# Expert passes in another order, weights in the mixers' scratch, and a ranking by small matmuls, in a two-block transformer kernel

## The chip, the core and the metric

The kernel runs on one core of a Trainium2 chip. A core has TensorE (PE, matmuls), VectorE (DVE), ScalarE (ACT), GpSimd (POOL) and SyncE (SP, which here issues nearly all transfers), an on-chip memory of 128 partitions (SBUF) and accumulation banks for matmuls (PSUM). Weights lie in the device's memory and are brought in by 16 DMA engines. The metric is the device time of one execution, in microseconds.

## What is computed

256 tokens of width 1024, in f32, go through two blocks. The first (attention or pooling, and a dense feed-forward) is not touched. The second has three token mixers with an output projection, then a mixture of 32 experts, then a gate with token inputs p:

```python
h = h + jnp.concatenate([ya, yb, yc], axis=-1) @ w_out[i]
h = h + hierarchical_moe(rms_norm_2(h, norm2_g[i]), router_gw[i], ...)
gate = jax.nn.sigmoid(rms_norm_2(h, ple_norm_g[i]) @ ple_gate_w[i])
h = h + gate * (p[i] @ ple_proj_w[i]).astype(F32)
return rms_norm_2(h, final_g)
```

The router takes the best of 4 groups for a token and in it the 2 best of 8 experts. Each expert has w_gate and w_up (1024 x 256) and w_down (256 x 1024), 1 MB each:

```python
g_top = jnp.argmax(g_logits, axis=-1)
e_val, e_loc = lax.top_k(e_in, TOP_K)
e_w = jax.nn.softmax(e_val, axis=-1) * g_w[:, None]
hb = jax.nn.silu(xb @ w_gate[e]) * (xb @ w_up[e])
yb = (hb @ w_down[e]) * wt[:, None]     # summed over a token's two experts
```

## The kernel before

The program runs `first_block`, then `second_mixers`, then `moe`. Engines run side by side, each in its own fixed order; semaphores hold an instruction until what it reads is there and what it overwrites has been read. A tile of a pool with the same name reuses the same buffer, so a load waits until the last reader of the former tile is done.

**Mixers.** `second_mixers` projects the tokens, runs the three mixers (scratch tiles kas, qa, sbt, uu, va and others) and multiplies with w_out (L1255). In its last stretch the rows are turned (L1282, L1324), and the router's logits are accumulated (L1283, L1325). `y_out` splits y into a high part (ACT, L1297) and a low part y - high (POOL, L1300), in two halves of 512 columns. Sixteen matmuls (L1344) multiply the token inputs p with ple_proj_w; their weights are loaded by L1267.

**Experts.** `moe` finds for each expert its tokens (one_hot, L1462, from the ranks rk), gathers their columns by matmuls with the one-hot matrix (`gather`, L1478, into xg, one gather for two passes) and works in passes (counted from 0) of 128 slots: the first matmuls of a pass (`hidden`, gate and up, L1588), the product with silu (L1594, ft), the turn of the hidden rows (L1616, into fh), the down projection (`down`, L1633), and the return to the tokens (`combine`, L1645, L1648). A pair holds two experts with 64 slots each, a quad four with 32 each. The first six experts (S) go by their number. The other 26 are ranked by their number of tokens: the six with most tokens (H) form pairs, the other 20 quads (Q). The order is SSSHHHQQQQQ: six pairs, five quads, eleven passes. Whatever does not fit in the slots is handled by an `If` after pass 7 (L1786), which reads a count nmi (L1748).

The ranking compares each of 26 counts with each (L1535 to L1545, 26 x 26 = 676 elements per partition on all 128 partitions), and puts ranks and weights of tokens in the new order (L1551, L1552). Its result `place` is read into a register of SP (L1406) for each load of a ranked expert.

**Loads.** `ExpertLoads.plan` lists 48 loads of 2 MB: (gate x, up x), (gate y, up y), (down x, down y) for a pair, six loads in the order gate, up, down for a quad. A load needs a place of 2 MB: three in the pool raw, three of whi and wlo, and at the start two of wx0 to wx3. `upto_pass(p, more)` issues loads up to so many beyond the end of pass p. All are issued by SP in program order (L1416), so a load that waits holds those behind it.

After the last pass a gate projection, sigmoid, the token inputs and a last norm end the kernel.

Of the kernel before, what the change touches and what calls it, by code (L numbers as in the profile page):

```python
# [19 lines left out]
P = 128  # L20
# [809 lines left out]
def w_consts(e, tp):  # L830
# [46 lines left out]
    def route():  # L877
# [6 lines left out]
        nc.gpsimd.memset(e.onb, 1.0)  # L884

# [32 lines left out]
def second_mixers(e, sp, ma, hx, xhi, xlo, racc):  # L918
# [3 lines left out]
    with tc.tile_pool(name="m2", bufs=1, reuse_waits="tile") as m2, banks(e, "psw", ps=3, z=3, py=1, px=1):  # L922
# [3 lines left out]
        kas = [m2.tile([P, 2, S], F32, name="ka%d" % j) for j in range(2)]  # L926
# [92 lines left out]
        def sgu_b():  # L1019
            vv = st["v"]  # L1020
            sq = m2.tile([P, 8, 64], F32, name="wd3")
# [39 lines left out]
        def sb1(i, s):  # L1061
# [5 lines left out]
            t = m2.tile([P, S + P], F32, name="sbt", bufs=3)  # L1067
# [13 lines left out]
        def sb3(i, s):  # L1081
# [8 lines left out]
            if s == 1:  # L1090
                if i == 0:
                    st["ya", 0] = m2.tile([P, S], F32, name="ya")
                elif i == 1:
                    t = m2.tile([P, 2, S], F32, name="vv")
                    st["ya", 1], st["ya", 2] = t[:, 0], t[:, 1]
# [61 lines left out]
        def ml3(h0, h1):  # L1157
            if h0 == 0:
                st["yb"] = m2.tile([P, 2, 384], F32, name="va")
# [11 lines left out]

        def p_load():
            st["p"] = [m2.tile([P, S], F32, name="qa", bufs=2) for _ in range(2)]
            for b in range(2):
                nc.gpsimd.dma_start(st["p"][b], a["p_2"][0, 0, b * P:(b + 1) * P])

        def p_turn():
            ps = bank(e, "z", [P, 2, S])
            for k in range(2):
                for b in range(2):  # L1180
                    nc.tensor.transpose(ps[:, k, b * P:(b + 1) * P], st["p"][b][:, k * P:(k + 1) * P], e.ident)
            e.pT = [e.tmp.tile([P, L], F32, name="acc2", bufs=2) for _ in range(2)]
            for k in range(2):
                nc.scalar.activation(e.pT[k][:, :S], ps[:, k], AF.Copy)
# [13 lines left out]
        u = st["u"] = m2.tile([P, 2, 256], F32, name="uu")  # L1198
# [7 lines left out]
        va = st["va"] = m2.tile([P, 2, 384], F32, name="va")  # L1206
# [9 lines left out]
        for i in range(3):  # L1216
            ps = col(("qa", i))
            qa = st["qa", i] = m2.tile([P, S], F32, name="qa", bufs=2)
# [13 lines left out]
        for f in (L_(sb1, 2, 1), L_(sb2, 2, 0), L_(sb3, 1, 1)):  # L1232
            f()
        plan_ = {
            (0, 0): [L_(decay, 3), L_(sb2, 2, 1), L_(sb3, 2, 0)], (0, 1): [L_(sb3, 2, 1), p_load],
            (1, 0): [ya_norm], (1, 1): [L_(conv_act, 0), L_(conv_act, 1)],
            (2, 0): [L_(ml1, 0), L_(ml1, 1), ya_out], (2, 1): [L_(conv_act, 2), L_(ml2, 0), L_(ml2, 1)],
            (3, 0): [L_(ml1, 2), p_turn], (3, 1): [L_(ml2, 2), L_(conv_act, 3)],
# [21 lines left out]
        for n in range(7):  # L1260
# [24 lines left out]
        def squares(ps, i0, i1, n):  # L1285

            for b in range(2):
                jk = m2.tile([P, 512], F32, name="wd3")
                nc.scalar.activation(jk[:, :(i1 - i0) * P], ps[b], AF.Square, accum_out=ssy[:, b, n:n + 1])

        def y_out(c, late=None):

            q = slice(c.start // KT, c.stop // KT)
            turned = lambda t, b: t[:, b].rearrange("p (k q) -> p k q", k=KT)[:, :, q]
            for b in range(2):
                src = y[:, b, c].rearrange("p (q k) -> p k q", k=KT)
                i = nc.scalar.activation(turned(yh, b), src, AF.Copy)  # L1297
                if late:
                    queue(e, i, late)
                nc.gpsimd.tensor_sub(turned(yl, b), src, fr(turned(yh, b)))  # L1300

        for i in range(KT + 2):
# [9 lines left out]
            if i == 6:  # L1312
# [3 lines left out]
                y_out(slice(0, 512))  # L1316
# [20 lines left out]

        e.pp = e.xs.tile([P, 2, D], F32, name="hs")
        for b in range(2):
            for hf in range(2):  # L1340
                c = slice(hf * 512, hf * 512 + 512)
                ps = bank(e, "z")
                for k in range(2):
                    nc.tensor.matmul(ps, e.pT[k][:, b * P:(b + 1) * P], e.proj[:, k, c], start=(k == 0), stop=(k == 1))  # L1344
# [564 lines left out]
```

## Time and profile before

| | us |
|---|---|
| median of 3 runs | 971.07 (969.52 to 971.22) |
| the profiled execution, device time | 970.93 |
| its span, first to last instruction | 969.1 |
| PE busy | 893.7 (92%) |
| DVE busy | 546.1 (56%) |
| ACT busy | 433.9 (45%) |
| POOL busy | 107.7 (11%) |

The device time is 1.83 us longer than the span, which covers only instructions. A busy share over the whole span mixes stages with different limits: 206.94 MB are read, 216 GB/s as a mean, but the rate changes from stage to stage, and so does what an engine waits for. Times below are counted from the start of the span. The first block ends near 530, the mixers near 677, the experts near 930.

### The profile page before, as it was taken

The page shows a single profiled execution, that of the slowest core. Times are in us where ns is not written, and L with a number is a line of the kernel's source. Part 1 is how long each engine was busy: PE and PEld are TensorE (multiplying, and loading weights), DVE is VectorE, ACT ScalarE, POOL GpSimd, SP SyncE. Part 2 cuts the span into 40 slices and gives each one's busy share as a digit, 9 for nine tenths or more (in the row PEclk, how much of TensorE's full clock was granted, in tenths as well). Part 3 has the DMA queues.
Part 4 walks back from the last instruction along what each step waited for, and adds up shares of the span by engine and source line. Part 5 has one row for each costly group of instructions (what it writes and reads, how often), then busy time and mean ns, then how long its engine had stood idle before and what let it go on. Part 6 is the DMA issues. An engine that isn't in the chain of part 4 may idle for free. (4 is left out here: it accounts for less than half of the span.)

```text
span 969.1 us, 16636 instructions
## 1 busy us (share of the span) xinstructions
PE 893.7 (92%) x6709; PEld 762.4 (79%) x6709; DVE 546.1 (56%) x1041; ACT 433.9 (45%) x800; POOL 107.7 (11%) x154
## 2 busy tenths in 40 slices
PE   7899999999999899999998899999799997778795
PEld 5799999998886899999998798899556563334355
DVE  7985555445998786655445755694933322221255
ACT  5564443435774574444433656564321220201155
POOL 3400000021400360000021310001100000000001
PEclk9899999999999999999999999999999997978898
DMA  7659543466332557553476135078795899999951
GB/s 233 208 174 217 175 147 120 127 216 248 121 111 88 174 124 226 179 171 120 130 234 220 65 118 182 7 260 303 295 385 228 357 414 417 419 415 415 412 180 44
DMA packets 110324, 210.24 MB, mean 217 GB/s; under 512 B 3660, under 2 KB 85776, under 8 KB 102048
## 3 DMA queue, kind: packets, MB, share of 16 engines
q1 hardware_dynamic: 108464, 204.91, 58.8%
q0 software_dynamic: 1488, 3.68, 2.1%
q8 instruction: 54, 0.88, 0.4%
q10 hardware_dynamic: 288, 0.52, 0.1%
q14 instruction: 30, 0.25, 0.1%
HBM read 206.94 MB, written 2.16 MB: 216 GB/s over the span
## 5 line engine op out<-in xcount | busy, mean ns | idle before, releaser
L315 DVE TENSOR_TENSOR wlo<-raw,whi 128x1024 fp32r<-128x1024 f32 (+4 forms) x151 | 213.9, 1420 | 119.8 <-ACT whi L315 119.4
L328 PE MATMUL ps<-xhi,whi 128*128 128x256 f32 (+1 forms) x912 | 261.6, 289 | 8.1 <-ACT xhi L319 5.3
L315 ACT ACTIVATE whi<-raw 128x1024 fp32r<-128x1024 f32 (+4 forms) x151 | 181.4, 1202 | 193.1 <-PE ps L328 188.8
L328 PE MATMUL ps<-xlo,whi 128*128 128x256 f32 (+1 forms) x912 | 261.7, 287 | 2.4 <-DVE xlo L320 1.9
L328 PE MATMUL ps<-xhi,wlo 128*128 128x256 f32 (+1 forms) x912 | 260.1, 285 | 0.0
L328 PEld LDWEIGHTS ps<-xhi,whi 128*128 128x128 f32 x912 | 173.4, 191 | 11.0 <-ACT xhi L319 6.1
L328 PEld LDWEIGHTS ps<-xlo,whi 128*128 128x128 f32 x912 | 173.9, 191 | 3.6 <-DVE xlo L320 2.6
L328 PEld LDWEIGHTS ps<-xhi,wlo 128*128 128x128 f32 x912 | 174.0, 191 | 0.0
L328 PE MATMUL ps<-hhi,whi 128*128 128x272 f32 (+1 forms) x352 | 100.9, 287 | 0.0
L328 PE MATMUL ps<-hhi,wlo 128*128 128x272 f32 (+1 forms) x352 | 100.4, 285 | 0.0
L328 PE MATMUL ps<-hlo,whi 128*128 128x272 f32 (+1 forms) x352 | 100.4, 285 | 0.0
L400 POOL TENSOR_TENSOR acc<-acc,sq 128x272 f32<-128x272 f32 (+1 forms) x24 | 34.6, 1442 | 373.0 <-ACT sq L394 372.6
L1594 DVE SCALAR_TENSOR_TENSOR ft<-ps,ws,ft 128x256 f32<-128x256 f32 x11 | 5.3, 483 | 114.8 <-PE ps L1588 79.8
L328 PEld LDWEIGHTS ps<-hhi,whi 128*128 128x128 f32 x352 | 66.9, 190 | 0.1
L328 PEld LDWEIGHTS ps<-hlo,whi 128*128 128x128 f32 x352 | 66.9, 190 | 0.1
L328 PEld LDWEIGHTS ps<-hhi,wlo 128*128 128x128 f32 x352 | 66.9, 190 | 0.0
L1588 PE MATMUL ps<-raw,xg 128*32 128x256 f32 (+1 forms) x512 | 51.5, 440 | 11.3 <-DMA raw<-in_w_up_dram 11.3
L1588 PEld LDWEIGHTS ps<-raw,xg 128*32 128x32 f32 (+1 forms) x512 | 30.4, 136 | 30.8 <-DMA raw<-in_w_up_dram 15.4
L1588 PE MATMUL ps<-whi,xg 128*32 128x256 f32 (+1 forms) x224 | 41.0, 456 | 9.6 <-ACTq L1786 5.8
L320 DVE SCALAR_TENSOR_TENSOR yl<-ps,ws,yh 128x512 fp32r<-128x512 f32 x22 | 16.5, 751 | 55.9 <-ACT yh L319 55.9
L423 DVE TENSOR_TENSOR ft<-ps,rpre 128x272 f32<-128x272 f32 (+1 forms) x44 | 18.8, 431 | 51.1 <-PE ps L328 51.0
L1588 PE MATMUL ps<-wlo,xg 128*32 128x256 f32 (+1 forms) x224 | 39.2, 453 | 5.1 <-DMA wlo<-in_w_gate_dram 5.1
(548 smaller groups left out, 1597.3 us busy)
## 6 DMA issues: line engine op xcount, KB each, us to landing
raw<-in_w_gate_up_dram SPq DMA_DIRECT2D x44, 1024.0 KB
raw<-in_w_up_dram SPq DMA_DIRECT2D x26, 1024.0 KB
raw<-in_w_down_dram SPq DMA_DIRECT2D x16, 1408.0 KB
raw<-in_w_down_dram SPq DMA_DIRECT2D x16, 1024.0 KB
whi<-in_w_gate_dram SPq DMA_DIRECT2D x14, 1024.0 KB
wlo<-in_w_gate_dram SPq DMA_DIRECT2D x10, 1024.0 KB
wlo<-in_w_down_dram SPq DMA_DIRECT2D x8, 1024.0 KB
whi<-in_w_down_dram SPq DMA_DIRECT2D x8, 1024.0 KB
```

What stands on the lines that cost most here:

```text
L315: return e.nc.scalar.activation(hi, src, AF.Copy), e.nc.vector.tensor_sub(lo, src, fr(hi))
L320: e.nc.vector.scalar_tensor_tensor(lo, src, g, fr(hi), op0=ALU.mult, op1=ALU.subtract))
L328: e.nc.tensor.matmul(ps, w(k), x(k), start=(first and n == 1), stop=(last and n == 3 * nk))
L400: nc.gpsimd.tensor_add(st["acc"][:, :n], st["acc"][:, :n], sq[:, :n])
L423: nc.vector.tensor_mul(t[:, :n], pss[0][:, :n], r[:, :n])
L1588: s.last = nc.tensor.matmul(pg[j][s.c * x:s.c * x + s.c], s.xg[:, k, s.s0 + x * s.c:s.s0 + (x + 1) * s.c], ws[x, j][:, k], start=(k == 0), ...
L1594: s.gated = nc.vector.scalar_tensor_tensor(t, pg[1], sc, t, op0=ALU.mult, op1=ALU.mult)
```

## The change

In words, in the order of the program:

- Some scratch of the mixers (kas, qa, sbt, u, va and one square) moves into two tiles wx0 and wx1 of the pool ma. Load 0 of the experts goes into these, and is issued by the mixers' plan behind the last use of sbt and va. With four tiles wx2 to wx5 of the pool mo for two more loads there are nine places for loads 0 to 17, seven for 18 to 31 and six from 32 on (`place_of`).
- `upto_pass` issues a load when the load before it in its place belongs to a pass that is over.
- The order of the passes is SSSQHQHQHQQ. Passes of one gather may now be a pair and a quad (`one_hot` with runs).
- The load of ple_proj_w and of p moves from the mixers behind pass 7, their matmuls from the mixers behind pass 8 (`token_inputs`, before pass 9).
- The low part of the second half of y moves from POOL to DVE, behind the one-hot of the first gather. That gather takes all high parts first and then the low parts.
- The ranking works on 26 partitions, with counts turned by a matmul against ones. Ranks and weights are turned (`by_expert`) and put in order by a matmul with the permutation (`in_place`). What only later passes need (`others`: weights in order, the count nmi) goes behind the first pass's turn. The small tiles of the router lie in one tile.
- ft and fh have one buffer instead of two; xg lies in two tiles of different pools.

```diff
+        w0, w1 = [ma.tile([P, 2048], F32, name="wx%d" % j) for j in range(2)]
+        kas = [w0[:, 512 * j:512 * j + 512].rearrange("p (s c) -> p s c", s=2) for j in range(2)]
...
-            (0, 0): [L_(decay, 3), L_(sb2, 2, 1), L_(sb3, 2, 0)], (0, 1): [L_(sb3, 2, 1), p_load],
+            (0, 0): [L_(decay, 3), L_(sb2, 2, 1), L_(sb3, 2, 0)], (0, 1): [L_(sb3, 2, 1), e.ml.load],
...
             if n == 3:
-                e.proj, _ = [sp.tile([P, 2, D], F32, name=t) for t in ("whi", "wlo")]
-                nc.sync.dma_start(e.proj, a["ple_proj_w_2"][0].rearrange("(k p) f -> p k f", p=P))
+                e.ml.load()
...
-                nc.gpsimd.tensor_sub(turned(yl, b), src, fr(turned(yh, b)))
...
-        y_out(slice(512, D), r)
-        e.ml.load()
+        e.y_low = y_out(slice(512, D), r)
...
+ORDER = "SSSQHQHQHQQ"
+NPASS = len(ORDER)
...
+    def halves(self, i):
+        if 1 <= i < 4:
+            t = self.e.raw.tile([P, 2, 2048], F32, name="raw")
+            return [t[:, 0], t[:, 1]]
+        if 4 <= i < 7:
             return [self.sp.tile([P, 2048], F32, name=n) for n in ("whi", "wlo")]
+        pool, i = (self.e.ma, 0) if i == 0 else (self.e.mo, 2 * i - 12)
+        return [pool.tile([P, 2048], F32, name="wx%d" % (i + j)) for j in range(2)]
+    def place_of(self, j):
+        return j % 9 if j < 18 else (j - 18) % 7 if j < 32 else (j - 32) % 6 + 1
...
-    def upto_pass(self, p, more=0):
-        while self.n < min(len(self.plan), self.upto[p] + more):
+    def upto_pass(self, p, short=0):
+        while self.n < len(self.plan) - short and self.prior(self.n) < self.upto[p]:
             self.load()
...
+            first = q == 0
+            if first:
+                pss = [bank(e, "ps", [P, 2, 256]) for _ in part]
+                for h in (hnh, hnl):
...
+        chosen = e.found
+        with tc.issue_after(chosen.ins):
+            e.y_low(nc.vector)
...
-            t = scratch()
-            nc.vector.tensor_tensor(t, over(key), down_(key), op=ALU.is_gt)
-            nc.vector.tensor_reduce(rank, t, axis=AX.X, op=ALU.add)
-            nc.vector.scalar_tensor_tensor(sorted_, over(rank), 1.0, down_(io[:, :ND]), op0=ALU.add, op1=ALU.is_equal)
...
+            nc.vector.scalar_tensor_tensor(key, key, keyc, e.ones[:ND, :ND], op0=ALU.is_gt, op1=ALU.mult,
+                                           accum_out=rankc)
+            nc.vector.tensor_scalar(perm, io[:ND, :ND], rankc, 1.0, op0=ALU.subtract, op1=ALU.is_equal)
+            ps = bank(e, "ps", [P, ND])
+            nc.tensor.matmul(ps[:1], e.ioc[:ND, 1:2], perm, start=True, stop=True)
...
+        def by_expert(src, n):
+            ps = bank(e, "ps", [P, 2, P])
             for b in range(2):
-                t = scratch(b)
-                nc.vector.tensor_mul(t, sorted_, over(src[:, b, NS:]))
-                nc.vector.tensor_reduce(to[:, b, NS:], t, axis=AX.X, op=ALU.add)
+                nc.tensor.transpose(ps[:ND, b], src[:, b, NS:], e.ident)
+            nc.scalar.activation(byx[:, n], ps[:ND].rearrange("p b t -> p (b t)"), AF.Copy)
+        def in_place(to, n):
+            ps = bank(e, "ps", [P, 2, ND])
+            for b in range(2):
+                nc.tensor.matmul(ps[:, b], byx[:, n, b * P:(b + 1) * P], perm, start=True, stop=True)
+            nc.vector.tensor_copy(to[:, :, NS:], ps)
...
+        def token_inputs():
+            pT = mo.tile([P, 2, S], F32, name="wx4")
+            pp = e.pp = mo.tile([P, 2, D], F32, name="wx5")
...
+        MID, LATE = 7, 8
...
-        in_place(rkq, rk)
-        in_place(wtq, wt)
+        for _ in range(2):
+            e.ml.load()
+        def others():
+            in_place(wtq, 1)
...
             if p == 0:
-                for n in range(2):
-                    e.ml.load([mo.tile([P, 2048], F32, name="wx%d" % (2 * n + j)) for j in range(2)])
...
             if p < last:
-                e.ml.upto_pass(p, 8 if p < 2 else 6)
+                e.ml.upto_pass(p)
...
+            if p == LATE:
+                token_inputs()
             if p == MID:
...
+                proj = mo.tile([P, 2, D], F32, name="wx2")
+                nc.sync.dma_start(proj, a["ple_proj_w_2"][0].rearrange("(k p) f -> p k f", p=P))
+                pin = mo.tile([P, 2, S], F32, name="wx3")
+                nc.gpsimd.dma_start(pin, a["p_2"][0, 0].rearrange("(b p) f -> p b f", p=P))
```

On SP, before, where the loads pass from static to ranked experts (wx2, wx3: load 7; raw_7688: load 8; raw_7691: load 9; nmi and place are reads into registers):

```order
L1416 DMA wx2_7684<-in_w_gate_2_dram 128x2048
L1416 DMA wx3_7685<-in_w_up_2_dram 128x2048
L1416 DMA raw_7688<-in_w_down_2_dram 128x2x1024 x2
L1748 TENSOR_LOAD nmi_7585
L1748 ISA x2
L1406 TENSOR_LOAD place_7530
L1406 ISA x2
L1416 ISA
L1416 DMA raw_7691<-in_w_gate_2_dram 128x2048
```

On SP now at the same place (wx4, wx5: load 8; wx0_7640, wx1_7641: load 9):

```order
L1424 DMA wx4_7494<-in_w_down_2_dram 128x2x1024
L1424 DMA wx5_7495<-in_w_down_2_dram 128x2x1024
L1414 TENSOR_LOAD place_7453
L1414 ISA x2
L1424 ISA
L1424 DMA wx0_7640<-in_w_gate_2_dram 128x2048
L1414 TENSOR_LOAD place_7453
L1414 ISA x2
L1424 ISA
L1424 DMA wx1_7641<-in_w_gate_2_dram 128x2048
L1826 TENSOR_LOAD nmi_7586
L1826 ISA x2
```

The read of nmi moved from ahead of load 9 to behind it, and the loads are one further: load 8 is the one in the last new place.

On SP, before, near the end of the mixers (raw_6467 and raw_6531: w_out; raw_6854: load 0; raw_6964: load 1):

```order
L148 DMA raw_6467<-in_w_out_2_dram 128x2x1024 x2
L148 DMA raw_6531<-in_w_out_2_dram 128x2x1024 x2
L1416 DMA raw_6854<-in_w_gate_2_dram 128x2048
L1416 DMA raw_6854<-in_w_up_2_dram 128x2048
L1416 DMA raw_6964<-in_w_gate_2_dram 128x2048
L1416 DMA raw_6964<-in_w_up_2_dram 128x2048
```

On SP now (raw_6461 and raw_6524: w_out; wx0_6701 and wx1_6702: load 0; raw_6844: load 1):

```order
L148 DMA raw_6461<-in_w_out_2_dram 128x2x1024 x2
L1424 DMA wx0_6701<-in_w_gate_2_dram 128x2048
L1424 DMA wx1_6702<-in_w_up_2_dram 128x2048
L148 DMA raw_6524<-in_w_out_2_dram 128x2x1024 x2
L1424 DMA raw_6844<-in_w_gate_2_dram 128x2048
L1424 DMA raw_6844<-in_w_up_2_dram 128x2048
```

Load 0 moved ahead of the second load of w_out.

On DVE, before, the ranking (key: counts; yh and so: 26 x 26 comparisons; gt, wp and ws belong to pass 0):

```order
L1535 SCALAR_TENSOR_TENSOR key<-ps,io 128x26
L1514 CAST wsp<-wt 128x3x2 x2
L1537 TENSOR_TENSOR yh<-key 128x676
L1515 TENSOR_TENSOR wsp<-wt,wsp 128x3x2 x2
L1538 TENSOR_REDUCE rank<-yh 128x26
L1601 CAST gt<-ps 128x256
L1539 SCALAR_TENSOR_TENSOR so<-rank,io 128x676
L1607 COPY wp<-ps 128x6
L1541 TENSOR_TENSOR yh<-so,io 128x676
L1609 TENSOR_TENSOR ws<-wp 128x3
L1551 TENSOR_TENSOR yl<-so,rk 128x676
```

On DVE now, from the selection slb on (tri_le: the ranks; qb: the low part of y; yl: small tiles; rankc and perm: ranks and permutation):

```order
L1462 TENSOR_TENSOR slb<-slb,yl 128x64
L1470 SCALAR_TENSOR_TENSOR tri_le<-ps,slb 128x64
L1491 TENSOR_TENSOR G<-io,tri_le 128x256 x2
L1291 TENSOR_TENSOR qb<-xlo,xhi 128x8x64 x2
L1581 SCALAR_TENSOR_TENSOR yl<-ps,io 26x26
L1583 SCALAR_TENSOR_TENSOR yl<-ps,ioc 26x1
L1544 TENSOR_TENSOR yl<-lgg,yl 128x8
L1547 TENSOR_TENSOR yl<-yl 128x8
L1585 SCALAR_TENSOR_TENSOR yl,rankc<-yl,ones 26x26
L1569 CAST wsp<-ss_7329 128x3 x2
L1587 TENSOR_SCALAR perm<-io,rankc 26x26
```

The operations of 676 elements are gone; the low part of y stands behind the one-hot G, and the ranking is done before the weights of the tokens.

## Rows read from the trace of the kernel before

**Rows 1.** The chain of waits: start, us, engine, line, tile

```profile
913.01 14.00 DMA wlo<-in_w_down_dram
...
927.05 3.62 PE ps L1633 x20
```

**Rows 2.** Stages: width, then PE, PEld, DVE, ACT, POOL busy, PEclk, DMA share, GB/s

```profile
767.00:927.00 160.00, 131.53 (x1066) 66.46 (x1065) 37.23 (x85) 26.04 (x53) 0.00 (x0) 0.88 1.02 412
...
699.00:767.00 68.00, 65.07 (x435) 41.11 (x434) 22.68 (x68) 16.94 (x33) 0.55 (x1) 0.97 0.79 310
...
636.00:699.00 63.00, 58.97 (x444) 52.17 (x442) 45.90 (x131) 30.45 (x69) 7.37 (x15) 0.97 0.77 292
...
600.00:630.00 30.00, 30.00 (x199) 26.41 (x198) 16.95 (x31) 16.28 (x27) 0.84 (x4) 1.00 0.02 5
```

**Rows 3.** Slices of 10 us, same columns

```profile
730.00:740.00 10.00, 10.00 (x70) 5.84 (x67) 4.56 (x13) 1.54 (x3) 0.00 (x0) 1.00 0.30 125
...
740.00:750.00 10.00, 10.00 (x83) 7.80 (x79) 3.06 (x6) 1.55 (x3) 0.00 (x0) 1.00 0.71 245
...
810.00:820.00 10.00, 7.00 (x64) 2.96 (x64) 0.00 (x0) 0.47 (x1) 0.00 (x0) 0.67 1.01 417
```

**Rows 4.** Waits of SP's queue: released by, us in total, times, longest

```profile
SPq L1416 <- PE ps L1588: 64.9, 12, 14.6
...
SPq L1416 <- PE ps L1633: 49.2, 12, 15.6
...
SPq L1748 <- DVE wp L1610: 4.3, 1, 4.3
```

**Rows 5.** SP's issues (loads 8 and 9): start, us

```profile
699.06 0.89 SPq L1416 DMA_DIRECT2D raw<-in_w_down_dram  x2
...
705.45 0.37 SPq L1416 DMA_DIRECT2D raw<-in_w_gate_dram  x1
```

**Rows 6.** Line L1089: duration ns, first and last start

```profile
L1089 PE MATMUL py<-sbt,va x12: 272/273/273, 590.6 to 620.2; 128*64 128x128 f32 x12
```

**Rows 7.** PE around the router and pass 0: start, us, [idle before]

```profile
676.34 5.40 PE L1344 MATMUL z<-whi,acc 128*128 128x512 f32 x12
...
684.78 0.19 PE L1445 MATMUL ps<-slb,ltb 128*128 128x32 bf16 x1 [3.05 <-DVE slb L1443]
...
691.91 7.18 PE L1588 MATMUL ps<-raw,xg 128*64 128x256 f32 x64
...
701.85 0.44 PE L1616 MATMUL ps<-ident,ft 128*128 128x128 f32 x2 [2.76 <-DVE ft L1594]
```

**Rows 8.** DVE around the router and in the ranking

```profile
679.07 0.16 DVE L1515 TENSOR_TENSOR wsp<-ss,wsp 128x3 fp32r<-128x3 f32 x1
...
679.62 1.48 DVE L1515 TENSOR_TENSOR wsp<-ss,wsp 128x3 fp32r<-128x3 f32 x1
...
681.16 1.47 DVE L1362 TENSOR_TENSOR ge<-ge,gi 128x8 f32<-128x8 f32 x1
...
693.39 0.86 DVE L1551 TENSOR_TENSOR yl<-so,rk 128x676 f32<-128x676 f32 x1
```

**Rows 9.** POOL around the router

```profile
679.56 3.04 POOL L1300 TENSOR_TENSOR qb<-xlo,xhi 128x512 fp32r<-128x512 f32 x2 [2.72 <-ACT xhi L1297]
```

**Rows 10.** Tile xlo on DVE: ns min, median, max

```profile
L1649 DVE TENSOR_TENSOR xlo<-xlo,ps x44: 674/679/689, 716.0 to 933.9; 128x512 f32<-128x512 f32 x44
```

**Rows 11.** PE, hidden matmuls of passes 3, 5, half of 6 (from 0)

```profile
740.41 7.13 PE L1588 MATMUL ps<-raw,xg 128*64 128x256 f32 x64
...
772.86 7.13 PE L1588 MATMUL ps<-raw,xg 128*64 128x256 f32 x64
...
795.42 3.83 PE L1588 MATMUL ps<-raw,xg 128*32 128x256 f32 x63
```

**Rows 12.** Lines L1344 and L1786

```profile
L1344 PE MATMUL z<-whi,acc x16: 592/592/676, 673.0 to 681.1; 128*128 128x512 f32 x16
...
L1786 PEldq COMPARE_BRANCH  x1: 6107/6107/6107, 839.6 to 839.6; - x1
```

More of the change, by code (lines that the diff above doesn't have):

```diff
@@ L1336, in second_mixers, with first_max @@
                                                op0=ALU.mult, op1=ALU.add)
[L1338 to L1344, printed above, removed]
[L1345 to L1350 removed]
+        e.y_low = y_out(slice(512, D), r)
+def first_max(e, small, src, n, iota):
     nc = e.nc
     m = src.shape[1]
[L1354 removed]
+    mx = small(m)
     nc.vector.tensor_reduce(mx, src, axis=AX.X, op=ALU.max)
[L1356 removed]
+    eq = small(m, n)
     nc.vector.tensor_tensor(eq, src, mx[:, :, None].to_broadcast([P, m, n]), op=ALU.is_equal)
@@ L1368, with passes @@
 PAIRS = (NS + NH) // 2
-NPASS = PAIRS + (ND - NH) // 4
+ORDER = "SSSQHQHQHQQ"
+NPASS = len(ORDER)
+def passes():
+    at = {"S": 0, "H": NS, "Q": NS + NH}
+    for c in ORDER:
+        n = 4 if c == "Q" else 2
+        yield at[c], n
+        at[c] += n
+PASS = list(passes())
 class ExpertLoads:
@@ L1465, in one_hot @@
-            return G[:, :, :n * c]
-        def gather(G, n, xg=None, part=range(KT // 2)):
-            if xg is None:
-                xg = mo.tile([P, KT, 256], F32, name="xg", bufs=2)
+            part = PASS[2 * q:2 * q + 2]
+            runs = [(0, x, n, P // n) for x, n in part[:1]]
+            for x, n in part[1:]:
+                if (x, n) == (runs[0][1] + n, runs[0][2]) and x != NS:
+                    runs = [(0, runs[0][1], 2 * n, P // n)]
+                else:
+                    runs.append((P, x, n, P // n))
@@ new lines, in one_hot, with gather, out @@
+            for s0, x0, n, c in runs:
+                r = rk if x0 < NS else rkq
+                for b in range(2):
+                    e.found = nc.vector.tensor_tensor(
+                        G[:, b, s0:s0 + n * c].rearrange("p (x c) -> p x c", c=c),
+                        io[:, None, :c].to_broadcast([P, n, c]),
+                        r[:, b, x0:x0 + n, None].to_broadcast([P, n, c]), op=ALU.is_equal)
+            return G[:, :, :P * len(part)]
+        def gather(G, xg=None, part=range(KT // 2), q=0):
+            n = G.shape[2]
+            if xg is None:
+                xg = e.xs.tile([P, KT, 256], F32, name="hs") if q % 2 == 0 else mo.tile([P, KT, 256], F32, name="xg")
+            def out(k2, ps):
+                for d in range(2):
+                    k = 2 * k2 + d
+                    nc.scalar.activation(xg[:, k, :n], ps[:, d, :n], AF.Copy, scale=e.g2[:, k:k + 1])
+            first = q == 0
+            if first:
+                pss = [bank(e, "ps", [P, 2, 256]) for _ in part]
+                for h in (hnh, hnl):
+                    for k2, ps in zip(part, pss):
+                        for d in range(2):
+                            k = 2 * k2 + d
+                            for b in range(2):
+                                nc.tensor.matmul(ps[:, d, :n], h[:, b, k * P:(k + 1) * P], G[:, b],
+                                                 start=(h is hnh and d == b == 0), stop=(h is hnl and b == 1),
+                                                 skip_group_check=True)
+                        if h is hnl:
+                            out(k2, ps)
+                return xg
@@ L1683, in overflow @@
                 p = Pair(2, lambda x, j: load(KT, gus[j][x, bass.ds(i, 1)]), lambda x: load(2, dns[x, bass.ds(i, 1)]),
-                         gather(G, 2 * C, xg), 0, [G[:, b] for b in range(2)], [wq[:, b] for b in range(2)], place)
+                         gather(G, xg, q=1), 0, [G[:, b] for b in range(2)], [wq[:, b] for b in range(2)], place)
                 p.slots()
@@ L1759, in moe @@
             cur.turn()
+            if p == 0:
+                with tc.issue_after(cur.last.ins):
+                    most = others()
             if prev:
```

265 lines of the change are left out of this document (136 added, 129 removed).

## Prediction

> **What bounds the kernel now.** I read the chain of waits from its end, then the busy table by stage, then the waits of SyncE's queue, then single rows. The chain ends in weights: the last two down projections land at 927.05 us, and from there 42.05 us of matmuls, norms and gate lead to the end of the span [rows 1]. The stage table shows what those weights waited for. From 767 to 927 the transfers run at 412 GB/s with their engines full, and TensorE has work for 131.5 of 160 us. From 699 to 767 they run at 310 GB/s, from 636 to 699 at 292, and from 600 to 630 at 5 [rows 2]. So the last part is bound by bytes and the middle part is not: around 735 us the rate falls to 125 GB/s while TensorE is busy all the time [rows 3]. SyncE there waits for places: it waited 64.9 us for hidden matmuls (L1588) and 49.2 us for down matmuls (L1633) to release buffers [rows 4]. Six pairs in a row give TensorE much work for few bytes, then five quads the reverse.
>
> The experts' weights are 48 loads of 2.097 MB. After load 8 goes out at 699.06 [rows 5], 40 loads and one 2.1 MB gate load remain until the last landing: 86.0 MB, which at 412 GB/s is 208.7 us. It took 927.05 - 699.06 = 228.0. **So 19.3 us of transfer time are lost.** The stage table gives nearly the same: (412 - 310) x 68 us = 6.9 MB, or 16.8 us [rows 2].
>
> **The change, part by part.** I follow the landing of the last down projection, and keep the 42.05 us behind it: the last quads, the gate loads and the final matmuls are ordered as before.
>
> *Load 0 early.* The scratch that now also holds load 0 is read last by the matmuls of L1089, at 620.2 + 0.27 us [rows 6]. The transfer falls into the stage with 5 GB/s [rows 2] and is down before the next entry of SyncE is due. Nothing waits behind it. So nine loads are done or under way at the end of the first hidden pass, where there were eight: 2.1 MB less later, 5.1 us.
>
> *The router.* The low part of y went through GpSimd, 3.04 us for two instructions [rows 9]; beside it two tiny operations of VectorE take 1.48 and 1.47 us, and their like takes 0.16 before it [rows 8]. Both lie ahead of the selection (slb) for which TensorE idles [rows 7]. With the low part on VectorE behind the one-hot they should shrink, 1.3 us each: 2.6 us. The low part then costs VectorE two operations of this shape at 0.68 us [rows 10], 1.4 us; the sixteen gather matmuls of the high part now run first and cover it. Uncovered it costs at most 1.4. Of the 16 token-input matmuls (0.59 us each [rows 12]) that leave, four stand among the last output matmuls and could bring up to 2 us more; I take 0, as TensorE waits for sums there anyway. The other twelve filled TensorE while the router ran [rows 7]; without them it idles longer and may run the gather at half clock, up to 2 us. So the first hidden pass, which ended at 699.09, ends at **T = 696.5**, bounds 694.5 and 699.1.
>
> [...]
>
> *Ranking by matmuls.* Eleven VectorE operations of 676 elements, 0.85 us each [rows 8], become transposes, a few tiny matmuls and operations on 26 partitions: about 9 us off VectorE. TensorE waited 2.76 us for VectorE's ft before the first turn [rows 7]; that goes, and the first down pass ends some 2.5 us earlier. The new matmuls are under 0.3 us each on TensorE, ten of them, against that. On the path of the bytes it only releases load 2's place earlier, inside the idle count below. I take 0, bounds -2.5 and +2.
>
> *The read of the overflow count on SyncE.* Before, load 9 waited 4.3 us behind it [rows 4, 5]. Now load 9 goes out with T, and the count is read behind it; it comes out of the first turn, some 6 us after T. One load covers 5.1 us, so about 1 us stays idle, counted below.
>
> *The order SSSQHQHQHQQ and nine places.* Two consecutive passes with their gather keep TensorE 32.45 us: the hidden matmuls of the fourth and the sixth pass start at 740.41 and 772.86 with no idle between [rows 11]. A quad's half takes 3.83 us [rows 11], two halves 7.7 against 7.13, so a quad weighs about what a pair weighs. In bytes a pair is 3 loads, 15.3 us at 412 GB/s, and a quad 30.5. Before, the pairs gave TensorE 32.45 us for 30.5 us of bytes with six or eight places: hence the gaps. A pair and a quad together are 45.8 us of bytes against 32.45 of TensorE, so from the fourth pass on every place is free before the transfers need it. Only the three first pairs can starve them. There the places come free so, by an estimate from 32.45 us for two passes and from the first down pass: two at T, one at T + 6.5, two at T + 13.6, one near T + 26, two at T + 33.4. Load 9 runs from T, load 10 from the count at T + 6.2 (1 us idle), load 11 behind it, 12 and 13 from T + 16.4, 14 from T + 26.6 to T + 31.7, then 1.7 us idle until the third hidden pass ends. By the same walk the old order loses 3.0, 1.3, 9.1, 2.0 and 4.5 us, together 19.9 (the trace has 19.3). To the 2.7 us of the new one I add 3.3 for hand-offs that come late: **6 us idle**, bounds 3 and 14.
>
> *Token inputs moved.* Their 1.3 MB (proj and p) leave the stage with spare transfers and enter the full one: +3.2 us, certain if that stage is full. Their TensorE work is 16 x 0.59 = 9.4 us at most, behind the ninth pass, together with the wait for p and proj on TensorE's in-order queue. The pair-and-quad surplus of 45.8 - 32.45 = 13.3 us hides it; without that cover it costs the 9.4. I take 1.5, bounds 0 and 6. The overflow test after the eighth pass held TensorE's loader for 6.1 us [rows 12] and still stands there, under the same cover.
>
> **Sum.** From T there remain 39 loads (81.8 MB), 1.3 MB of token inputs and 2.1 MB of gate: 85.2 MB, 206.8 us at 412 GB/s. 696.5 + 206.8 + 6 idle = 909.3, where the 1.5 for token inputs lies within the 3.3 of margin; I use 909. The landing is 18 us earlier than 927.05. The profiled execution took 970.93 us, so the forecast is 970.93 - 18 = 952.9; the median of the three runs is 0.14 higher: **953**. By parts: load 0 gives 5.1, T 2.6, the idle time 13.3, the token inputs take 3.2; that is 17.8.
>
> **Rivals.**
> - *Full gain.* T at 694.5 and only 3 us idle: 5 us better, **948**. For it: the gaps of before are all waits for places. Against: three pairs still come first.
> - *Partly filled.* The third and fourth pass still starve the transfers, or the token inputs hold up TensorE's queue so that places come late: idle 14 instead of 6, **961**. For it: the first passes run at TensorE's pace, and the count is read on the queue that issues every load.
> - *It doesn't fill.* Places of the new order are released no faster than before, so 19 us stay idle, and only load 0 and T are gained, less the token inputs: about **967 to 970**. Against it: the row around 735 us names the place, not the transfer, as what was late.
> - *Slower: TensorE's clock.* The pair-quad rhythm needs 32.45 us at full clock in 45.8. From 810 to 820 the granted clock was 0.67 while quads waited for weights [rows 3]. If the waits within each pass keep the clock down in the new rhythm, TensorE becomes the bound: below 32.45 / 45.8 = 0.71 of full clock it costs time, and below 0.64 the whole 18 us are lost over the three and a half pair-quad rounds ((32.45 / 0.64 - 45.8) x 3.5 = 17). [...] Against it: over the whole stage from 767 on the mean granted clock was 0.88 with TensorE only 82% busy [rows 2], and a clock that falls leaves fewer waits, which lifts it again.
>
> [...]
>
> **How the numbers follow.** Forecast 0.55 (949 to 957), full gain 0.15, partly filled 0.18, not filled 0.05, slower 0.07. A measurement of this kernel tells about 0.2% (2 us) from no change. Faster: 0.55 + 0.15 + 0.18, and a little less than half of the fourth: 0.90; same 0.03; slower 0.07. The range of 8 in 10 takes the forecast, most of the full gain and most of the partly filled case: 945 to 962.
>
> **What would show it.** In the new profile: one 2 MB load between 620 and 630; slb some 2.6 us earlier and no VectorE operation of 1.4 us beside it; load 9 leaving at the end of the first hidden pass; no 10 us slice between 710 and 900 under some 380 GB/s except near the third pass; SyncE's waits for L1588 and L1633 shorter; last down projection near 909; 42 us behind it. I am wrong if slices under 300 GB/s remain after 750, if the granted clock of the stage falls under 0.7, if TensorE waits at the token inputs with SyncE behind it, or if the tail grows.

## The result and the profile after

The changed kernel takes 954.72 us (median of 4, 953.86 to 955.34), the kernel before, measured beside it, 970.97 (969.52 to 971.22): a ratio of 0.9835, 95% interval 0.9818 to 0.9852. The forecast was 953, the range 945 to 962. The span of the profiled execution is 953.7.

The busy table by stage, the answer to [rows 2] (us, PE, PEld, DVE, ACT, POOL busy, PEclk, DMA share, GB/s; the limits are moved as the forecast had it, measured are a first release at 697.77 and a last landing at 911.37):

```profile
767.00:909.00 142.00, 120.87 (x981) 65.02 (x978) 33.16 (x74) 27.44 (x57) 0.72 (x1) 0.93 1.01 411
...
695.00:767.00 72.00, 70.76 (x578) 46.77 (x576) 25.81 (x84) 16.99 (x36) 0.55 (x1) 0.98 0.94 376
...
636.00:695.00 59.00, 51.53 (x421) 49.32 (x422) 39.73 (x130) 29.03 (x65) 4.47 (x14) 0.91 0.79 309
...
600.00:630.00 30.00, 30.00 (x194) 26.40 (x193) 15.73 (x29) 15.19 (x27) 0.20 (x2) 1.00 0.24 82
```

The last stage is as full as before (411 GB/s) and, up to the measured landing, 15.7 us shorter. The stage in front of it went from 310 to 376 GB/s. Before 630 there is now some traffic: the first expert load.

Slices of 10 us with the same columns, those that are not full (the answer to [rows 3]):

```profile
690.00:700.00 10.00, 9.29 (x83) 6.99 (x81) 2.10 (x10) 2.93 (x9) 0.00 (x0) 1.00 0.33 108
...
700.00:710.00 10.00, 9.47 (x54) 5.13 (x55) 4.61 (x27) 1.76 (x3) 0.55 (x1) 0.83 0.87 319
...
730.00:740.00 10.00, 10.00 (x88) 5.65 (x87) 5.74 (x16) 2.23 (x4) 0.00 (x0) 1.00 0.99 386
...
870.00:880.00 10.00, 10.00 (x134) 6.97 (x130) 3.71 (x10) 1.92 (x6) 0.00 (x0) 1.00 0.92 358
```

The slice from 730 on has 386 GB/s where it had 125. What is left stands in the slices from 690 and 700, around the first release, and a little in the one from 870, behind the token inputs.

The waits of SyncE's queue (released by, us in total, times, longest), the answer to [rows 4]:

```profile
SPq L1424 <- PE ps L1643: 53.5, 10, 13.7
...
SPq L1424 <- PE ps L1688: 21.9, 8, 5.5
...
SPq L1826 <- DVE G L1491: 4.6, 1, 4.6
```

Lines L1643 and L1688 are the former L1588 and L1633. The waits for hidden matmuls fell from 64.9 to 53.5 us, those for down matmuls from 49.2 to 21.9. The wait for the count (L1826) is still there, now behind load 9.

The end of the chain of waits (start, us), the answer to [rows 1]:

```profile
897.39 13.93 DMA wlo<-in_w_down_dram
...
911.37 3.62 PE ps L1688 x20
```

The last down projection lands at 911.37 instead of 927.05, 15.7 us earlier; the 42.3 us behind it are the former 42.05.

### The profile page after: what moved, and what is told of

It reads as the page before. It is cut to its first block, busy times and chain, and to the rows that moved or that the text cites. A ratio compares the mean times of both kernels' runs of the same rounds, so it can differ in the third digit from the quotient of the medians.

```text
span 953.7 us, 16697 instructions
## 1 busy us (share of the span) xinstructions
PE 883.4 (93%) x6727; PEld 764.2 (80%) x6727; DVE 536.6 (56%) x1042; ACT 432.9 (45%) x801; POOL 106.3 (11%) x153
## 4 chain that ended last, share of the span: by engine, by line
PE 71%; DMA 15%; DVE 8%; ACT 3%; issue 1%; SPq 1%; POOL 0%; DVEq 0%; ACTq 0%; POOLq 0%
PE ps L328 50%; PE ps L1643 4%; DMA wlo<-in_w_down_dram 4%; DMA wx<-in_ple_proj_w_dram 2%; DMA raw<-in_w_down_dram 2%; DMA wlo<-in_w_up_dram 2%; DMA whi<-in_w_down_dram 2%; PE ps L1248 2%; PE ps L1688 2%; DVE hs L354 2%; PE ps L713 2%; DVE rt L351 2%; DVE xlo L320 1%; DMA wx<-in_w_gate_dram 1%; PE z L328 1%
## 5 line engine op out<-in xcount | busy, mean ns | idle before, releaser
L400 POOL TENSOR_TENSOR acc<-acc,sq 128x272 f32<-128x272 f32 (+1 forms) x24 | 34.7, 1445 | 374.0 <-ACT sq L394 373.6
L1643 PE MATMUL ps<-raw,hs 128*32 128x256 f32 (+1 forms) x288 | 34.7, 401 | 5.9 <-ACTq L1872 5.9
L76 ACT ACTIVATE ft<-ps,ws 128x256 f32<-128x256 f32 x11 | 5.2, 474 | 64.3 <-PE ps L1643 64.3
L319 ACT ACTIVATE yh<-ps,ws 128x512 fp32r<-128x512 f32 x22 | 15.1, 687 | 38.2 <-PE ps L1688 38.2
L367 POOL TENSOR_TENSOR acc<-acc,sq 128x272 f32<-128x272 f32 (+1 forms) x28 | 26.3, 941 | 50.8 <-ACT sq L366 50.1
```

What stands on the lines that cost most here:

```text
L367: e.mark = nc.gpsimd.tensor_add(acc[:, :n], acc[:, :n], sq[:, :n])
L400: nc.gpsimd.tensor_add(st["acc"][:, :n], st["acc"][:, :n], sq[:, :n])
L1643: s.last = nc.tensor.matmul(pg[j][s.c * x:s.c * x + s.c], s.xg[:, k, s.s0 + x * s.c:s.s0 + (x + 1) * s.c], ws[x, j][:, k], start=(k == 0), ...
```

## The experiments

Each is the changed kernel with one edit, or with those named, timed in five rounds beside the kernel before on one chip. That kernel's median was 971.7 to 972.4 in these groups and 970.97 beside the changed kernel, so ratios are compared across groups, and times only beside them. A difference of under 0.2% (2 us) is not told apart.

**Order and places.** The prediction gave one sum, 13.3 us, to the new order and the nine places together. Three runs split it.

e1_old_order:

```diff
-ORDER = "SSSQHQHQHQQ"
+ORDER = "SSSHHHQQQQQ"
```

> The changed kernel with the passes in the old order, SSSHHHQQQQQ; places, loads, router and ranking stay as changed. Theory (the order fills the transfers): the three hot pairs run at TensorE's pace again and the transfers idle some 9 to 12 us more between 740 and 800, so the last down projection lands about 11 us later: 965 to 967. Rival (the extra places alone do it): within 2 us of the changed kernel's 954.7.

Measured: 960.08 us, ratio 0.9874 (0.9855 to 0.9894). The order is worth about 0.4% or 4 us (0.0039, known to about 0.002), under half of what was expected; the extra places keep much of the gain without it. The slice with the idle transfers:

```profile
780.00:790.00 10.00, 10.00 (x123) 5.70 (x123) 1.50 (x2) 3.81 (x8) 0.00 (x0) 1.00 0.48 163
```

TensorE is busy for the whole slice while the transfers run at 163 GB/s: no load goes out between 775.52 and 788.68, while TensorE works on the last pair and the first quad.

e10_six_new:

```diff
-        return j % 9 if j < 18 else (j - 18) % 7 if j < 32 else (j - 32) % 6 + 1
+        return j if j < 9 else (j - 9) % 6 + 1
```

> The changed kernel with its order SSSQHQHQHQQ, nine loads ahead as changed, but from load 9 on only the six places of raw, whi and wlo. With the next run it splits the gain in idle time into order and places. Theory (both are needed; a quad's six loads fill all six places, so the transfers wait at each pass that ends): +8 to +10 us, 963 to 965. Rival (the order alone does it): within 2 us of 954.7.

Measured: 964.70 us, ratio 0.9926 (0.9913 to 0.9940).

e11_six_old has this edit and that of e1_old_order.

> The same six places from load 9 on, with the old order SSSHHHQQQQQ. Theory (neither order nor places): the idle time of the kernel before comes back in full, less the ninth load and the earlier router, plus the token inputs in the full stage: 968 to 973. If order and places add up, it lies 5 us (what the old order cost with all places) above the run with six places and the new order.

Measured: 968.97 us, ratio 0.9973 (0.9959 to 0.9986). Two of its slices, and one of e10_six_new:

```profile
730.00:740.00 10.00, 10.00 (x69) 6.33 (x68) 5.60 (x14) 2.23 (x4) 0.00 (x0) 1.00 0.70 255
...
740.00:750.00 10.00, 10.00 (x80) 8.03 (x78) 3.61 (x10) 2.12 (x6) 0.00 (x0) 1.00 0.40 147
```

```profile
730.00:740.00 10.00, 10.00 (x104) 5.51 (x106) 5.75 (x16) 2.27 (x5) 0.00 (x0) 1.00 0.56 210
```

Both have full TensorE and transfers at 147 to 255 GB/s around 735, as in [rows 3]. The four ratios form a square: old order 0.9973 with six places and 0.9874 with nine, new order 0.9926 and 0.9835. The order gives 0.0047 or 0.0039, the places 0.0099 or 0.0091. Each of these is known to about 0.002, and within that they add up: together 0.0138, or 13.4 us. That is the 13.3 of the prediction; about two thirds of it are the places.

**The ninth load.** e2_ninth_late:

```diff
-        return j % 9 if j < 18 else (j - 18) % 7 if j < 32 else (j - 32) % 6 + 1
+        return (j + 1) % 9 if j < 18 else (j - 17) % 7 if j < 32 else (j - 32) % 6 + 1
...
-            (0, 0): [L_(decay, 3), L_(sb2, 2, 1), L_(sb3, 2, 0)], (0, 1): [L_(sb3, 2, 1), e.ml.load],
+            (0, 0): [L_(decay, 3), L_(sb2, 2, 1), L_(sb3, 2, 0)], (0, 1): [L_(sb3, 2, 1)],
...
-        for _ in range(2):
+        for _ in range(3):
             e.ml.load()
```

> The changed kernel, but no load goes into the mixers' scratch while the mixers run: the ninth load goes out with the seventh and eighth, after the mixers. Nine places as before. In the profile of the changed kernel the transfers idle from about 692 to 698. Theory A (the early load is worth its 5.1 us, as the prediction had it): 959 to 960. Theory B (the place is what counts; the ninth load fits into the idle time ahead of the first release): 954.7 within 1 us.

Measured: 954.70 us, ratio 0.9832 (0.9810 to 0.9854), no different from the changed kernel. e3_eight_places leaves the load out there altogether:

```diff
-        return j % 9 if j < 18 else (j - 18) % 7 if j < 32 else (j - 32) % 6 + 1
+        return j % 8 + 1 if j < 16 else (j - 16) % 7 if j < 30 else (j - 30) % 6 + 1
...
-            (0, 0): [L_(decay, 3), L_(sb2, 2, 1), L_(sb3, 2, 0)], (0, 1): [L_(sb3, 2, 1), e.ml.load],
+            (0, 0): [L_(decay, 3), L_(sb2, 2, 1), L_(sb3, 2, 0)], (0, 1): [L_(sb3, 2, 1)],
```

> The changed kernel with eight loads ahead of the first hidden pass instead of nine: the mixers' scratch holds no weights until load 16. Theory (one load less done at the first release costs one load's time): +5 us, 959 to 960. Rival (the transfers have idle time later that takes it in): 955 to 956.

Measured: 960.24 us, ratio 0.9881 (0.9863 to 0.9900), 0.0046 or 4.5 us above the changed kernel. In the traces the way from the first release to the last landing is 218.2 us, against 213.6. So the ninth load is worth about its 5.1 us, but because a place for it exists, not because it goes out early: the gap ahead of the first release takes it in. The slice before that release in e2_ninth_late and in e3_eight_places:

```profile
690.00:700.00 10.00, 8.89 (x76) 6.74 (x74) 1.81 (x12) 2.04 (x6) 0.00 (x0) 1.00 0.27 81
```

```profile
690.00:700.00 10.00, 9.29 (x81) 7.00 (x79) 2.10 (x10) 2.20 (x7) 0.00 (x0) 1.00 0.18 52
```

Even with the ninth load issued late there is still idle time ahead of the release.

**The count.** e4_count_late moves the read of nmi from the first turn to the end of the third pass:

```diff
-            return nc.values_load(nmi[0:1, 0:1], min_val=0, max_val=S)
+            return nmi
...
-                    most = others()
+                    nmi = others()
...
+            if p == 2:
+                most = nc.values_load(nmi[0:1, 0:1], min_val=0, max_val=S)
             if p == LATE:
```

> The changed kernel with the overflow count read by SyncE after the third pass instead of behind load 9. Theory A (the 2 us that load 10 waits for the count are lost): 952 to 953. Theory B (they are lost anyway a little later, when the third pass's place comes free and load 15 waits for it): 954.7 within 0.7 us.

Measured: 954.73 us, ratio 0.9824 (0.9808 to 0.9840). The issue of load 10 and the slice in which the third pass frees places:

```profile
700.08 1.47 SPq L1424 DMA_DIRECT2D raw<-in_w_gate_dram  x2
```

```profile
730.00:740.00 10.00, 10.00 (x91) 5.48 (x90) 5.74 (x16) 2.23 (x4) 0.00 (x0) 1.00 0.91 345
```

Load 10 goes out at 700.08 instead of 705.28, and the slice from 730 falls from 386 to 345 GB/s. From load 9 to the last landing it is 213.9 us, against 213.6: what load 10 gains comes back as idle time at later places, as in the walk of the prediction, and the count costs nothing that the time shows.

**The token inputs.** e7_no_tokens loads neither p nor ple_proj_w, leaves their matmuls out and uses zeros:

```diff
-            pT = mo.tile([P, 2, S], F32, name="wx4")
-            pp = e.pp = mo.tile([P, 2, D], F32, name="wx5")
...
+            e.pp = mo.tile([P, 2, D], F32, name="wx5")
+            nc.gpsimd.memset(e.pp, 0.0)
```

> The changed kernel without the token inputs: neither p nor ple_proj_w is loaded, their matmuls are left out and zeros stand for their product. Theory (1.3 MB in the full stage cost 3.2 us, the wait of TensorE for them at pass 9 up to 1.5 more): 950 to 951.5. Rival (they are hidden): 954 to 955.

Measured: 950.89 us, ratio 0.9790 (0.9770 to 0.9810). The move of the token inputs into the full stage costs some 4 us, known to about 2. In the trace it is 210.5 us from load 9 to the last landing instead of 213.6, which is the time of the bytes (3.2) alone. In the changed kernel TensorE waits for them (start, us, [idle before]):

```profile
859.34 2.90 PE L1760 MATMUL ps<-wx,wx 128*128 128x512 f32 x3 [2.55 <-DMA wx<-in_ple_proj_w_dram]
```

**The router.** e5_low_pool gives the second low part back to GpSimd:

```diff
-        e.y_low = y_out(slice(512, D), r)
+        y_out(slice(512, D), r)(nc.gpsimd)
...
-        with tc.issue_after(chosen.ins):
-            e.y_low(nc.vector)
```

> The changed kernel with the low part of the second half of y on GpSimd again, at the end of the mixers. Theory (beside GpSimd two small operations of VectorE ahead of slb take 1.4 us longer each, and all loads follow the first hidden pass): slb and everything behind it 2 to 2.6 us later, 956.5 to 957.5. Rival (the two operations of 2.1 us that VectorE is now spared make up for it, or the idle transfers do): 954.7 within 0.7.

Measured: 956.63 us, ratio 0.9837 (0.9822 to 0.9852). By the ratio it can't be told from the changed kernel. The trace tells it: two rows of VectorE, one of GpSimd and the wait for slb in this run, and the like of the two rows of VectorE in the changed kernel:

```profile
679.49 1.62 DVE L1345 SCALAR_TENSOR_TENSOR yl<-yl,io 128x64 f32<-128x64 f32 x2
...
681.30 1.28 DVE L1568 TENSOR_TENSOR wsp<-ss,wsp 128x3 fp32r<-128x3 f32 x1
```

```profile
679.41 1.54 POOL L1291 TENSOR_TENSOR qb<-xlo,xhi 128x512 fp32r<-128x512 f32 x1 [1.52 <-ACT xhi L1294]
```

```profile
684.88 0.21 PE L1464 MATMUL ps<-slb,ltb 128*128 128x32 bf16 x1 [9.13 <-DVE slb L1462]
```

```profile
680.33 0.30 DVE L1345 SCALAR_TENSOR_TENSOR yl<-yl,io 128x64 f32<-128x64 f32 x2
...
680.25 0.16 DVE L1570 TENSOR_TENSOR wsp<-ss,wsp 128x3 fp32r<-128x3 f32 x1
```

The long operations are back while GpSimd works (1.62 for a row of two and 1.28 us, where the changed kernel has 0.30 and 0.16), and slb comes later with them: TensorE waits 9.13 us for it instead of 6.67. Counted from the issue of w_q in the first block, which the change does not touch, the first hidden pass starts 2.6 us later than in the changed kernel (467.5 against 464.9); 0.5 of these lie in the mixers, 2.1 behind the last matmul of the router's logits.

e6_rank_cost adds the VectorE time that the old ranking took:

```diff
+            jr = small(ND)
+            for _ in range(11):
+                nc.vector.tensor_reduce(jr, y[:, 0, :ND * ND].rearrange("p (r x) -> p r x", x=ND), axis=AX.X, op=ALU.add)
```

> The changed kernel with eleven more operations of 26 x 26 elements on VectorE after the weights of the tokens, the amount that the ranking by matmuls took away (9.4 us). Their results are not used. Theory (they end beside the first hidden pass, and the transfers wait for that pass alone): 954.7 within 1 us. Rival (VectorE's ft and the ranked places come later, and all loads with them): +2.5 or more.

Measured: 957.95 us with a wide spread (953.0 to 959.57), ratio 0.9847 (0.9828 to 0.9866): inconclusive as a time. In the trace the added work is not hidden (start, us, [idle before]):

```profile
691.06 0.24 PE L1663 MATMUL ps<-wsp,G 128*128 128x6 f32 x1 [2.17 <-DVE wsp L1570]
```

TensorE waits 2.17 us for weights that VectorE makes, just ahead of the hidden matmuls. In this place the added operations are on the path; the old ranking stood partly behind that point, so the run doesn't tell what it cost.

**TensorE's share.** e9_pe_double does the hidden matmuls of passes 3 to 10 twice:

```diff
+                if not s.single and s.x0 >= NS:
+                    again = lambda o: [c for c in o if c[0] < 8] + o
+                    if s.nx == 4:
+                        order = again(order[:4 * KT]) + again(order[4 * KT:])
+                    else:
+                        order = again(order)
```

> The changed kernel with the hidden matmuls of passes 3 to 10 done twice on the same data (7.1 us more of TensorE in each pass), so that a pair and a quad need 32.45 + 14.3 = 46.7 us of TensorE at full clock beside 45.8 us of transfers. It stands for TensorE's clock falling to 0.7. Theory (below that point TensorE's work is free): +2 to +7 us, 957 to 962; for the doubled matmuls behind the last landing 3 to 4 of these. Rival (TensorE is on the path in every pass already): 14 us a round, over +35, above 990.

Measured: 977.34 us, ratio 1.0061 (1.0048 to 1.0074), between the two. The last landing is 21 us later, at 932.35. A slice of it and the longest waits of TensorE from 690 on:

```profile
780.00:790.00 10.00, 10.00 (x192) 5.98 (x184) 0.75 (x1) 0.91 (x2) 0.00 (x0) 1.00 0.28 98
```

```profile
PE ps L1649 <- ACTq L1878: 6.1, 1, 6.1
...
PE ps L1694 <- DMA wlo<-in_w_down_dram: 0.7, 1, 0.7
```

TensorE hardly waits for weights any more (0.7 us at most), and the transfers wait for it. Its granted clock in that slice is 1.00. Three starts of a quad's hidden pass, and between the last two the hidden pass of the pair behind the overflow test (a row can be cut at the edge of a window):

```profile
779.63 0.41 PE L1649 MATMUL ps<-wx,hs 128*32 128x256 f32 x2
...
824.01 6.25 PE L1649 MATMUL ps<-raw,xg 128*32 128x256 f32 x112
...
854.43 5.92 PE L1649 MATMUL ps<-raw,hs 128*64 128x256 f32 x26 [6.13 <-ACTq L1878]
...
885.91 0.40 PE L1649 MATMUL ps<-whi,hs 128*32 128x256 f32 x1
```

A round of a quad and a pair takes 44.4 us, not 46.7 and less than the 45.8 of its bytes, so by that sum the rounds alone would cost nothing. The round with the overflow test and the token inputs takes 61.9, which is 17.5 more: 6.1 in which TensorE stands still, 2.9 by which the hidden pass behind that is longer (the granted clock is 0.67 from 850 to 860 and 0.99 from 860 to 870), 8.5 for the token inputs. All this had been under the same cover and comes out when it is gone. It is not the whole: from load 9 to the last landing it is 237.2 us, 23.6 more than in the changed kernel. Between 780 and 840 the transfers lose some 11 us too, while TensorE is busy all the time; which places they wait for there was not tested.

e12_by_expert was meant as a better kernel: the hidden matmuls of a pair one expert after the other, so that a place is free half a pass earlier, with the edit of e4_count_late.

```diff
-                elif s.nx == 4:
-                    order.sort(key=lambda o: o[2])
+                else:
+                    order.sort(key=lambda o: o[2] if s.nx == 4 else o[1])
```

> The changed kernel with the count read after the third pass and the hidden matmuls of pairs ordered by expert, so that the first expert's gate and up place is free half a hidden pass (3.6 us) earlier. Theory (all time behind the first hidden pass follows from when the first place is free): load 9 goes out 3.6 us earlier into idle transfers, 950.5 to 952. Rival (the gain comes back as idle time at the third pass): 954 to 955.

Measured: 977.08 us, ratio 1.0055 (1.0037 to 1.0073). Both theories fall. The first expert's matmuls in the first pass:

```profile
690.54 6.47 PE L1643 MATMUL ps<-wx,hs 128*64 128x256 f32 x29
```

29 matmuls take 6.47 us, 0.22 us each. With the experts taking turns, 64 take 7.18 us, 0.11 each. The hidden pass of a pair nearly doubles (13.2 us). TensorE is busy in every slice from 710 to 850 and waits for weights for 6.1 us in all; until 760 the transfers wait for it, with 242 GB/s from 730 to 740. What the earlier release is worth can't be seen.

e13_warm adds to this kernel nine matmuls while TensorE waits for slb:

```diff
+        idle = bank(e, "z")
+        for _ in range(9):
+            nc.tensor.matmul(idle, e.ident, y[:, 0, 384:896], start=True, stop=True)
```

> The run before with nine matmuls of 128 x 512 on TensorE, results not used, between the router's last matmul and slb, where TensorE idles for 6.7 us. In the changed kernel the first sixteen gather matmuls then take 0.23 us each, the next sixteen 0.14. Theory (the idle time lowers the clock, and the first hidden pass sets all loads): the gather is 1.5 to 2 us shorter, and the time as much less than in the run before. Rival (the pass waits for VectorE's low part instead): no difference.

Measured: 977.68 us, ratio 1.0050 (1.0032 to 1.0068), no difference in time. From 676 to 684 the granted clock is 1.00 instead of 0.64 (this run, then the changed kernel, columns of the stage table):

```profile
676.00:684.00 8.00, 7.31 (x25) 3.33 (x24) 5.65 (x37) 2.98 (x7) 1.44 (x10) 1.00 1.01 428
```

```profile
676.00:684.00 8.00, 1.05 (x13) 0.81 (x12) 5.85 (x36) 4.87 (x13) 3.22 (x11) 0.64 0.99 382
```

The gather in this run and in the changed kernel (start, us, [idle before]):

```profile
683.73 2.14 PE L1518 MATMUL ps<-G,xhi 128*128 128x256 f32 x16 [0.69 <-DVE G L1494]
```

```profile
683.26 0.21 PE L1464 MATMUL ps<-slb,ltb 128*128 128x32 bf16 x1 [6.67 <-DVE slb L1462]
...
684.40 3.75 PE L1515 MATMUL ps<-G,xhi 128*128 128x256 f32 x16 [0.68 <-DVE G L1491]
```

The first sixteen matmuls take 2.14 instead of 3.75 us. From the first router matmul behind slb to the first hidden matmul it is 6.9 us, 8.2 in e12_by_expert. But counted from the issue of w_q the first hidden pass starts at 464.3 in both. The nine added matmuls (18 rows in the trace) run until 682.8, and the router's matmul stands behind them:

```profile
675.77 7.03 PE L1331 MATMUL z<-xlo,ident 128*128 128x512 f32 x16
...
682.63 0.18 PE L1467 MATMUL ps<-slb,ltb 128*128 128x32 bf16 x1
```

It starts 1.3 us later than in e12_by_expert (457.4 against 456.1 from w_q). So what the clock gave back, the added matmuls had taken before, and the run does not tell what a gather at full clock is worth.

No run was faster than the changed kernel by more than the measurement tells, except the one that leaves work out.

## Why the prediction held, step by step

- *The lost 19.3 us.* Held. In the changed kernel load 9 goes out at 697.77 and the last weights land at 911.37, 213.6 us for 85.2 MB, which at 412 GB/s need 206.8. So 6.8 us are idle; the prediction took 6, of which 3.3 were a margin without a row behind it. The landing comes 2.4 us behind the 909 of the forecast, most of it because load 9 goes out at 697.77 and not at 696.5. Two rows of SyncE (loads 9 and 10), the answer to [rows 5]:

```profile
697.77 1.61 SPq L1424 DMA_DIRECT2D wx<-in_w_gate_dram  x2
...
705.28 1.44 SPq L1424 DMA_DIRECT2D raw<-in_w_gate_dram  x2
```

- *Order and places.* The sum held (13.4 against 13.3), its ground only in part. The prediction let the order free every place in time from the fourth pass on; the square shows one third for the order, two thirds for the places. The old order with all places was then expected to cost about 11 us more, and measured 4 (known to about 2).
- *Load 0 early.* The size held (4.5 against 5.1), the reason did not. The prediction put it down to the idle stage before 630; e2_ninth_late shows that the place counts, and that the moment is free.
- *The router.* The size held, by luck; the split did not. In the profile T is 698.2, not 696.5; 1.15 us of that lie in the first block, which is the same code, as the issue of w_q shows (before, then after):

```profile
224.98 4.49 SPq L148 DMA_DIRECT2D raw<-in_w_q_dram  x2
```

```profile
226.13 4.49 SPq L148 DMA_DIRECT2D raw<-in_w_q_dram  x2
```

Counted from there, the first hidden pass starts at 466.9 before and at 464.9 after, and at 463.6 to 464.3 in seven of the experiments that don't touch the router (465.0 in e4_count_late, 466.2 in e3_eight_places). The profiles that are late have a lower granted clock in the mixers: 0.83 as a mean from 540 to 550, where the kernel before and six of those seven have 1.00 (the seventh, e12_by_expert, has no figure there). Two matmuls there in the changed kernel and in e2_ninth_late:

```profile
545.62 1.22 PE L377 MATMUL px<-acc,ones 128*128 128x256 f32 x2 [2.43 <-POOL acc L367]
```

```profile
545.54 0.70 PE L377 MATMUL px<-acc,ones 128*128 128x256 f32 x2 [2.44 <-POOL acc L367]
```

The same two matmuls take 1.22 or 0.70 us. The split is read from the last stretch: the first rows that are turned and the last matmul of the router's logits, before (with the token-input matmuls that stood between them) and after:

```profile
668.30 0.27 PE L1282 MATMUL z<-ident,hs 128*128 128x128 f32 x1
...
673.03 1.10 PE L1344 MATMUL z<-whi,acc 128*128 128x512 f32 x2
...
674.86 1.10 PE L1344 MATMUL z<-whi,acc 128*128 128x512 f32 x2
...
676.20 0.31 PE L1325 MATMUL px<-rw,hs 128*128 128x36 f32 x2
```

```profile
669.98 0.27 PE L1274 MATMUL z<-ident,hs 128*128 128x128 f32 x1
...
676.28 0.31 PE L1322 MATMUL px<-rw,hs 128*128 128x36 f32 x2
```

This takes 6.3 us instead of 7.9: the four token-input matmuls that left bring 1.6, where the prediction took 0. From there to the router's matmul behind slb it is 7.0 instead of 8.6 [rows 7], again 1.6, where the prediction had 2.6. From that to the first hidden pass it is 7.8 instead of 7.1, where it took 0. So 1.6 + 1.6 - 0.7 = 2.5 stands for its 2.6. In e5_low_pool the low part alone is worth 2.1. VectorE takes 2.13 us for it, not 1.4, under the 3.75 of the gather's first sixteen matmuls. The low clock in the gather is not new: from 684 to 691 the granted clock was 0.76 before and is 0.68 now (0.50 from 687 to 689 before, from 684 to 688 now); in the hidden pass, from 692 to 698, it is 1.00 in both.
- *The token inputs.* The cost was inside the bounds, by the trace the bytes alone. One sign of being wrong that the prediction named did show, in little: TensorE waits at the token inputs, SyncE waits for TensorE behind them (13.7 us, its longest wait for a hidden pass), and the slice from 870 has 358 GB/s, under the 380 that was forecast, which is 1.3 us.
- *The count.* It costs nothing (e4_count_late): the time that load 10 gains is lost again behind it.
- *Ranking.* TensorE's wait for ft ahead of the first turn fell from 2.76 us [rows 7] to 0.71, as forecast. That it is worth 0 is not shown: e6_rank_cost is inconclusive.

```profile
699.81 0.44 PE L1671 MATMUL ps<-ident,ft 128*128 128x128 f32 x2 [0.71 <-DVE ft L1649]
```

- *The slower rival.* Its chance was low for a good reason (the granted clock from 767 to 909 is 0.93, before it was 0.88), but its turning point was put too far off. The starts of the hidden passes of the fourth and the sixth pass in the changed kernel:

```profile
737.89 0.41 PE L1643 MATMUL ps<-wx,xg 128*32 128x256 f32 x2
...
768.47 0.41 PE L1643 MATMUL ps<-wx,hs 128*32 128x256 f32 x2
```

A round takes 30.6 us there, with TensorE busy all the time, not the 32.45 that the prediction carried over from two pairs; so alone it would have cover down to 30.6 / 45.8 = 0.67. But e9_pe_double put seven doubled hidden passes, 6.9 us more each, ahead of the last one, 48 us in all, and 23.6 came out, so only some 25 were covered. Against 3.5 x 30.6 = 107 us of rounds that is a turning point near 107 / (107 + 25) = 0.81 of the full clock, not 0.71. This is an estimate: no run here lowered the clock.

## What to carry to other kernels

Where a stage is bound by bytes and the stage ahead of it by matmuls, count the transfer time lost between the first release of a buffer and the last landing. More places to load into and an order that mixes heavy and light passes both win it back, and here they add up. When slack of one engine is what hides several things, add these up against it before calling any of them free. Here an early start of a transfer was worth nothing, as a later idle gap would take it in; the place that it needs was worth one load. And a sum that comes out can hide terms that cancel: check each against a row.

## What the runs showed of the hardware

- Hidden matmuls with 64 columns (f32) of two experts, which write different halves of the 128 partitions, overlap in the trace: in the changed kernel two of them start within 0.06 us of each other, the next two 0.22 us later, so that 64 take 7.18 us, 0.11 us each. Where those of one expert stand in a row, which all write the same half, 29 take 6.47 us, 0.22 us each (e12_by_expert). A reorder that looks neutral nearly doubled the pass, from 7.18 to 13.2 us.
- Small operations of VectorE (3 to 64 columns) gave rows of 1.28 to 1.62 us beside an operation of GpSimd of 1.5 us (in the kernel before and in e5_low_pool), and of 0.16 to 0.30 without it.
- Where TensorE idled for 6.7 us in the router, the granted clock was 0.64 as a mean from 676 to 684 and 0.68 from 684 to 691, with 0.50 from 680 to 688; with matmuls in that time, whose results nobody reads (e13_warm), it was 1.00 from 676 to 690.
